# A column roll on one core: the bulk copy's DMA engines take neighbouring rows in place of rows four apart

## The chip, the core and the metric

The kernel runs on one core of one Trainium2 chip. The metric is the device time of one execution in microseconds (us). Lower is better. The core has 16 DMA engines; a DMA that an engine such as SP (SyncE) or ACT (ScalarE) issues goes into that engine's queue, and its packets are worked on by the DMA engines.

## What is computed

The reference rolls every row of an 8192 x 8192 float32 matrix to the right by 100 columns; what leaves a row on the right comes back on its left.

```python
def reference(x: np.ndarray, shift: int) -> np.ndarray:
    return np.roll(x, shift, axis=1)
```

With `shift` 100: out[r, 100:] = x[r, :8092] and out[r, :100] = x[r, 8092:]. Nothing is calculated. The matrix has 268.44 MB, all of which is read from HBM and written to it once. One row has 32,768 bytes, so rows follow each other at 32 KB in both x and out.

## The kernel before

Here s is 100, and a is 256 (line 20 rounds 100 up to 128, line 22 adds 128), so g = a - s is 156. The output's columns are split at a:

- **The bulk**, out[:, 256:8192], is copied straight from x[:, 156:8092], from HBM to HBM (line 43). That is 7936 columns or 31,744 bytes of each row. The rows are taken in 128 blocks of 64 (loop over c, line 39). Inside a block, four DMAs (loop over j, line 41) take 16 rows each: j = 0 and 2 are issued on SP, j = 1 and 3 on ACT (line 43, `engines[j % 2]`). The view of lines 34 and 35 says which 16 rows: its axis e, the outer one of the DMA, has 16 entries, one for each DMA engine. In the last four blocks each DMA is split into two halves of 3968 columns (line 40), so each of the two queues has 248 DMAs of 496 KB and 16 of 248 KB. There is nothing between these DMAs but the wait of a queue for its own earlier DMAs.
- **The heads**, out[:, :256], go through SBUF on the POOL (GpSimd) queue, in 16 groups of 512 rows (loop over k, line 67). A partition holds four rows. Line 72 loads the 256 elements of x that straddle the border between two rows, three times for each partition, into t; lines 73 and 76 load the two pieces that t lacks into h; the DVE (VectorE) copies of lines 74 and 77 bring the rest from t into h in the rolled order. After all loads were issued, line 80 stores the 16 tiles h.

The bulk and the heads write different columns, and no one waits for the other. Both use the same 16 DMA engines.

Rows that DMA j of block c takes, before: c * 64 + 4 * e + j for e = 0 to 15. Entry e's rows over the four DMAs of a block are therefore four in sequence, and neighbouring entries are four rows (128 KB) apart.

Of the kernel before, what the change touches and what calls it, by code (L numbers as in the profile page):

```python
# [1 line left out]

# [4 lines left out]


@with_exitstack
def kernel(  # L10
    ctx: ExitStack,
    tc: tile.TileContext,
    x: bass.AP,
    shift: int,
    out: bass.AP,
):
    nc = tc.nc
    n_rows, n_cols = x.shape
    s = shift % n_cols
    a = -(-s // 128) * 128  # L20
    if 0 < a <= 384 and a + 128 <= n_cols:
        a += 128
    g = a - s
    P = nc.NUM_PARTITIONS
    engines = [nc.sync, nc.scalar]
    n_chunks = 16
    rows = n_rows // n_chunks

    xm = x.rearrange("(c e j) w -> c j e w", e=16, j=4)
    om = out.rearrange("(c e j) w -> c j e w", e=16, j=4)
    if a < n_cols:
        blocks = n_rows // 64
        mid = (a + n_cols) // 256 * 128
        for c in range(blocks):
            parts = ((a, mid), (mid, n_cols)) if c >= blocks - 4 and a < mid else ((a, n_cols),)  # L40
            for j in range(4):
                for lo, hi in parts:
                    engines[j % 2].dma_start(out=om[c, j, :, lo:hi], in_=xm[c, j, :, lo - s:hi - s])
    if a == 0:
        return


    if a > 512:
        for i in range(n_chunks):
            r = slice(i * rows, (i + 1) * rows)  # L50
            nc.gpsimd.dma_start(out=out[r, :s], in_=x[r, n_cols - s:])
            if g > 0:
                nc.gpsimd.dma_start(out=out[r, s:a], in_=x[r, :g])
        return

    Q = 4  # L60
    n_st = n_rows // (P * Q)
    reads = ctx.enter_context(tc.tile_pool(name="reads", bufs=n_st))
    heads = ctx.enter_context(tc.tile_pool(name="heads", bufs=n_st))
    xt = x.rearrange("(k p q) c -> k p q c", q=Q, p=P)
    ot = out.rearrange("(k p q) c -> k p q c", q=Q, p=P)
    tiles = []
    for k in range(n_st):
        t = reads.tile([P, Q - 1, a], x.dtype)
        h = heads.tile([P, Q, a], x.dtype)
        lead = bass.AP(tensor=x.tensor, offset=(k * P * Q + 1) * n_cols - s,  # L70
                       ap=[[Q * n_cols, P], [n_cols, Q - 1], [1, a]])
        nc.gpsimd.dma_start(out=t[:], in_=lead, single_packet=True)  # L72
        nc.gpsimd.dma_start(out=h[:, Q - 1, :s], in_=xt[k, :, Q - 1, n_cols - s:], single_packet=True)  # L73
        nc.vector.tensor_copy(h[:, :Q - 1, :s], t[:, :, :s])  # L74
        if g > 0:
            nc.gpsimd.dma_start(out=h[:, 0, s:], in_=xt[k, :, 0, :g], single_packet=True)  # L76
            nc.vector.tensor_copy(h[:, 1:, s:], t[:, :, s:])  # L77
        tiles.append(h)
    for k, h in enumerate(tiles):
        nc.gpsimd.dma_start(out=ot[k, :, :, :a], in_=h[:], single_packet=True)  # L80


# [1 line left out]
_INS = ['x', 'shift']  # L84
_OUTS = [((8192, 8192), 'float32')]

_NUMBERS = {'shift': 100}


# [26 lines left out]
```

## Time and profile before

| | before |
|---|---|
| median of 3 runs | 817.31 us |
| lowest and highest | 817.02 and 818.74 us |
| profiled execution, its span | 813.9 us |
| instructions in the profile | 689 |
| DMA packets | 22277 |
| bytes moved by the DMA engines | 276.90 MB, mean 340 GB/s |

The profiled execution's own time is its span of 813.9 us, from the first instruction to the last; the runs' times include what lies around the span, 3.4 us between the span and the median. The page counts a byte that goes from HBM to HBM once in "bytes moved", and twice (read and written) in its line on HBM. Whole packets have 31,744 bytes; the many packets under 512 B are 4 bytes long and tell a semaphore that a DMA engine's share of a DMA is done.

The DMA rate over the span, in 40 equal slices of 20.3 us, from the page:

```profile
GB/s 314 346 340 344 353 346 350 344 351 344 346 355 346 345 362 354 353 357 354 355 355 349 342 335 331 335 332 325 335 328 332 334 337 334 332 337 332 334 314 293
```

The first slice holds the start; the last the end, where the queues run empty.

### The profile page before, as it was taken

How to read it: one execution, taken by the hardware profiler on the slowest of the kernel's cores; microseconds unless marked ns; L12 is line 12 of the kernel's file. 1: busy time of each engine (PE TensorE's matmuls, PEld its weight loads, DVE VectorE, ACT ScalarE, POOL GpSimd, SP SyncE). 2: the span in 40 equal slices, each digit the busy share in tenths (PEclk: the TensorE clock that was granted, in tenths of full speed). 3: DMA queues.
4: the chain of work that ended last, by engine and by line, in shares of the span. 5: the costliest groups of instructions: out<-in, count | busy, mean ns of one | idle time of the engine just before them, and what ended most of it. 6: DMA issues, size and time to landing. Idle time of an engine off the chain costs nothing. (4 is left out here: it accounts for less than half of the span.)

```text
span 813.9 us, 689 instructions
## 1 busy us (share of the span) xinstructions
DVE 12.0 (1%) x32; POOL 41.1 (5%) x68
## 2 busy tenths in 40 slices
DVE  0000000000000000000000000000000000000000
POOL 2000011111000100000000000000000000000000
DMA  9999999999999999999999999999999999999998
GB/s 314 346 340 344 353 346 350 344 351 344 346 355 346 345 362 354 353 357 354 355 355 349 342 335 331 335 332 325 335 328 332 334 337 334 332 337 332 334 314 293
DMA packets 22277, 276.90 MB, mean 340 GB/s; under 512 B 9472, under 2 KB 9728, under 8 KB 13824
## 3 DMA queue, kind: packets, MB, share of 16 engines
q1 hardware_dynamic: 8448, 130.04, 45.9%
q10 hardware_dynamic: 8448, 130.04, 44.3%
q0 software_dynamic: 5376, 16.78, 8.9%
q14 instruction: 5, 0.04, 0.0%
HBM read 268.44 MB, written 268.44 MB: 660 GB/s over the span
## 5 line engine op out<-in xcount | busy, mean ns | idle before, releaser
L80 POOL DMA_DIRECT2D out_dram<-h x16 | 11.4, 713 | 139.5 <-DMA out_dram<-h 92.5
L76 POOL DMA_DIRECT2D h<-in_x_dram x16 | 8.6, 540 | 158.4 <-DMA t<-in_x_dram 158.4
L72 POOL DMA_DIRECT2D t<-in_x_dram x16 | 12.2, 760 | 32.1 <-DMA h<-in_x_dram 31.3
L73 POOL DMA_DIRECT2D h<-in_x_dram x16 | 8.9, 558 | 32.7 <-DMA h<-in_x_dram 32.7
L74 DVE COPY h<-t 128x300 f32<-128x300 f32 x16 | 5.9, 367 | 268.4 <-DMA t<-in_x_dram 268.4
L77 DVE COPY h<-t 128x468 f32<-128x468 f32 x16 | 7.5, 468 | 0.0
L97 POOL MEMSET const-float32-0.0<- 128x1 f32 x1 | 0.1, 98 | 0.2 <-issue 0.2
L97 POOL MEMSET const-bfloat16-1.0<- 128x1 bf16 x1 | 0.1, 101 | 0.0
L97 POOL MEMSET const-float32-1.0<- 128x1 f32 x1 | 0.1, 98 | 0.0
L97 POOL MEMSET const-uint8-127<- 128x1 uint8 x1 | 0.1, 98 | 0.0
## 6 DMA issues: line engine op xcount, KB each, us to landing
out_dram<-in_x_dram ACTq DMA_DIRECT2D x248, 496.0 KB, 12.5
out_dram<-in_x_dram SPq DMA_DIRECT2D x248, 496.0 KB, 12.5
out_dram<-h POOLq DMA_DIRECT2D x16, 512.0 KB, 102.9
t<-in_x_dram POOLq DMA_DIRECT2D x16, 384.0 KB, 48.9
out_dram<-in_x_dram SPq DMA_DIRECT2D x16, 248.0 KB, 5.9
out_dram<-in_x_dram ACTq DMA_DIRECT2D x16, 248.0 KB, 5.9
h<-in_x_dram POOLq DMA_DIRECT2D x16, 78.0 KB, 41.9
h<-in_x_dram POOLq DMA_DIRECT2D x16, 50.0 KB, 47.2
```

The source lines that it names most:

```text
L72: nc.gpsimd.dma_start(out=t[:], in_=lead, single_packet=True)
L73: nc.gpsimd.dma_start(out=h[:, Q - 1, :s], in_=xt[k, :, Q - 1, n_cols - s:], single_packet=True)
L74: nc.vector.tensor_copy(h[:, :Q - 1, :s], t[:, :, :s])
L76: nc.gpsimd.dma_start(out=h[:, 0, s:], in_=xt[k, :, 0, :g], single_packet=True)
L77: nc.vector.tensor_copy(h[:, 1:, s:], t[:, :, s:])
L80: nc.gpsimd.dma_start(out=ot[k, :, :, :a], in_=h[:], single_packet=True)
L97: nc = _bacc.Bacc("TRN2", target_bir_lowering=False, num_devices=1)
```

## The change

Two lines are changed, both views of the bulk copy. The order of the axes j and e in the rows of a block is exchanged:

```diff
-    xm = x.rearrange("(c e j) w -> c j e w", e=16, j=4)
-    om = out.rearrange("(c e j) w -> c j e w", e=16, j=4)
+    xm = x.rearrange("(c j e) w -> c j e w", e=16, j=4)
+    om = out.rearrange("(c j e) w -> c j e w", e=16, j=4)
```

DMA j of block c now takes the rows c * 64 + 16 * j + e. Neighbouring entries e take neighbouring rows (32 KB apart), and an entry's next row, in the next DMA, is 16 rows (512 KB) on. Line 43, the number and size of the DMAs, the queues that they are issued on, their order and the heads are as before.

## The prediction

> **What bounds the kernel now.** I read the page's utilisation part first, then its part on DMA queues, then busy time by stretches, then the trace's packet records queue by queue.
>
> The page:
>
> ```profile
> DVE 12.0 (1%) x32; POOL 41.1 (5%) x68
> ...
> DMA  9999999999999999999999999999999999999998
> ...
> q1 hardware_dynamic: 8448, 130.04, 45.9%
> q10 hardware_dynamic: 8448, 130.04, 44.3%
> q0 software_dynamic: 5376, 16.78, 8.9%
> ...
> HBM read 268.44 MB, written 268.44 MB: 660 GB/s over the span
> ...
> out_dram<-in_x_dram ACTq DMA_DIRECT2D x248, 496.0 KB, 12.5
> out_dram<-in_x_dram SPq DMA_DIRECT2D x248, 496.0 KB, 12.5
> ```
>
> No compute engine matters (1% and 5%); the 16 DMA engines are occupied from the first slice to the last. The three queue shares add to 99%. q1 and q10 are the SP and ACT queues with the bulk copy of line 43, q0 is POOL's with the heads. So the kernel is the DMA engines' time, and that is the number of packets times how long one takes.
>
> The stretches (columns: the stretch, its length, DVE busy, POOL busy, tensor clock, DMA share, GB/s):
>
> ```profile
> 100.00:200.00 100.00, 5.26 (x14) 11.57 (x19) 1.00 1.00 349
> 200.00:300.00 100.00, 3.75 (x10) 11.23 (x17) 1.00 1.00 349
> 300.00:400.00 100.00, 0.00 (x0) 4.99 (x7) 1.00 1.01 354
> 400.00:500.00 100.00, 0.00 (x0) 0.71 (x1) 1.00 1.01 346
> 500.00:600.00 100.00, 0.00 (x0) 0.00 (x0) 1.00 1.00 331
> 600.00:700.00 100.00, 0.00 (x0) 0.00 (x0) 1.00 0.99 334
> ```
>
> The DMA share stays at 1.00 while the rate falls from about 349 to 333 GB/s when the heads end near 480 us. The packet records say why. A whole-row packet of 31,744 B takes 1.174 us at the least (27.0 GB/s for an engine), 1.30 us on average from 20 to 250 us and 1.51 us from 500 to 780 us. The engines are occupied, but not at their own speed: something behind them is. A bulk byte is read from HBM and written to HBM; a head's byte touches HBM on one side only, SBUF on the other. Counting bulk bytes twice and head bytes once, 40 us slices carry 651 to 671 GB/s of HBM traffic from 40 us to 800 us. By stage: up to 500 us, (339 + 349 + 349 + 354 + 346) / 5 = 347.4 GB/s in all, 16.78 MB / 500 us = 33.6 of it heads, so 2 x 313.8 + 33.6 = 661; from 500 to 700 us, 2 x 332.5 = 665. Three mixes (bulk with head loads, with head stores, alone) end at one figure within 0.6%. **The bound is HBM traffic at about 663 GB/s**, and 536.9 MB / 813.9 us = 660 is the whole kernel.
>
> The Trainium skill, HBM Reference, Specifications (TRN2), puts one HBM domain at about 716 GB/s; 660 is 92% of that, and the same bytes at 716 would give an estimated 750 us of span, some 753 us in all. The sum below does not use it.
>
> **The change part by part.** Profile to median: the profiled span is 813.9 us, the median of the runs 817.3, so 3.4 us lie around the span; I keep them.
>
> *Removed and added:* nothing. The instruction lists of both kernels are the same on every engine: 264 DMAs on SP, 264 on ACT, 64 on POOL, 32 copies on DVE. Each bulk DMA is still 16 rows, one row for each engine: the queue's 3,968 whole-row packets are 248 DMAs x 16, and each DMA has 16 landings. Sizes, shift and alignment inside a row are unchanged, so the packet count (8448 on a queue) and the 1.174 us floor stay. Issue cost stays: 0.51 us an issue, 264 on a queue, 135 us of 814, and SP waits 667 us in 260 waits for an earlier DMA, so issuing is covered five times over. Cost 0.
>
> *Moved: the rows.* Within each block of 64 rows, DMA j took rows j, j+4, ..., j+60; now it takes 16j to 16j+15. At one moment the two queues touched 32 rows spread over 2 MB of x and of out; now they touch 32 adjacent rows, 1 MB. Neighbouring engines stand 32 KB apart, before 128 KB. An engine that walked four adjacent rows (128 KB nearly in one piece) now steps 512 KB. Three possible costs:
>
> (a) *The loss of the four-row sequence.* If a jump cost something, the packet that begins a group of four would be longer than its followers. I linked packets end to start in the 500 to 780 us stretch (2,843 links of 2,935 packets): the durations four packets apart correlate with 0.004, those two apart with -0.010. A period of four is not there. I take 0 us. If all the scatter above the stretch's median hung on it the mean could move from 1.481 to 1.509, 2%; I keep that in the range.
>
> (b) *Engines meeting on the same part of memory, because rows are a power of two apart.* The start shows the engines in step, one queue after the other, at 128 KB: the first five rounds of 16 packets took 1.62, 1.23, 1.34, 1.52 and 1.37 us on average, the sixth 1.175. Apart from the cold first round and the fourth, this is faster than the free-running 1.51. So standing in step at a power of two is no visible evil at 128 KB; no row has 32 KB in bulk. The heads come nearest: their stores are 1 KB pieces at a 32 KB pitch, and 300 to 480 us, where they run, carries the same 657 to 671 GB/s. I take 0, ends in the rivals.
>
> (c) *Skew among engines.* The 16 landings of one bulk DMA lie some 5 to 7 us apart and four DMAs of a queue are in flight (12.5 us to landing against one every 3.06 us). An engine would have to run 12 us ahead to go idle; the DMA share is 0.99 to 1.00, so this is covered now and stays so unless the skew doubles. Cost 0.
>
> Sum: 813.9 + 0 + 3.4 = 817.3. The ceiling differs by 0.6% between the two stages though the row order in them is the same, so a new order may move it by as much: 0.6% of 814 is 5 us, 812 to 822. Within this band I lean to the slow side, since the ceiling's best slice (671) is 1.2% above its 663 mean and its worst (651) 1.8% below, and say **818**.
>
> **The rivals.**
>
> *B, slower: adjacent rows crowd one part of HBM.* If memory is dealt out by address bits above a row's 32 KB, 32 rows in 1 MB reach fewer parts than 32 rows in 2 MB, and packets that start together wait for one another. For it: packets are 0.34 us over their floor in the pure stage, so waiting is what the time is made of, and the first round, 16 packets within 0.83 us, took 1.62. Against it: (b), and that the engines soon drift out of step. Price: all rounds at 1.62 for 1.51 would be +7.3%, 877 us; the worst warm 40 us slice, 1.533 for 1.509, is +1.6%, 830. I take 830, the row of warm traffic. It decides from about 3% of the rounds meeting like the first (0.2% / 7.3%).
>
> *C, faster: the rows at 32 KB spread better than those at 128 KB.* With all engines on rows of one remainder mod 4, before may have used a quarter of what a low address bit deals out. For it: the same 0.34 us of waiting. Against: engines drift over several j, so all remainders occur already. Price: the best slice kept throughout, 671 GB/s, 536.9 MB / 671 = 800.1, with 3.4 us 803.5; the far end, every whole-row packet at its floor, 7,936 x (1.425 - 1.174) / 16 = 124 us off, 693. I take 803.5, the row that this traffic has reached. The Trainium skill, DMA: Bandwidth & Descriptors, Latency and other measured facts, has copies losing rate as the pitch between streams grows (207 GB/s at 512 KiB, 103 at 4 MiB) and infers that streams in step fall on the same channels; by that rule a smaller pitch can only help. The trace agrees only in that packets wait; its in-step rounds at 128 KB do not show the loss.
>
> *D, the change does not reach the hardware as described.* A packet record carries its queue, not its engine; if the rows were dealt to engines otherwise, nothing would change: 817.3. It ends in the forecast's band and is counted there.
>
> **How the numbers follow.** A measurement of this kernel can tell about 0.2% from no change (its runs span 817.02 to 818.74): 815.7 to 818.9. The forecast (ceiling unmoved, with D) has 0.52, of which 0.20 falls within 0.2%, 0.13 faster, 0.19 slower, by the lean above. B has 0.28: the price of waiting is large and only some collisions are needed. C has 0.20: it needs headroom that only 1.2% of slices' scatter shows. Faster 0.13 + 0.20 = 0.33, same 0.20, slower 0.19 + 0.28 = 0.47. Both signs hold much, so: the forecast's own range is 812 to 822; the whole range goes from just past C's 803.5 to halfway into B's tail, 800 to 845, and leaves out about 0.09 on either side (C towards 693, B towards 877).
>
> **What would show it.** Right: after's pure stage (500 to 700 us) again at 331 to 335 GB/s, q1 and q10 again 45 and 44% in 8448 packets each, DMA digits 9 throughout, the heads ending near 480 us. B: the same DMA share with under 329 GB/s in the pure stage, the mean whole-row packet over 1.53 us. C: over 337 GB/s there, shorter packets. A DMA share well under 1.00 would show (c) wrong; a period of four in packet times, (a). What makes the forecast wrong is above all that HBM's ceiling is not a property of the traffic's volume but of its order, which no stage of before varies in bulk.

## The result, and the profile after

The kernel with the new row order takes **820.99 us** (median of 6 runs, 819.4 to 822.63) against 817.16 us before (6 runs, 816.08 to 818.74): ratio 1.0045, 95% interval 1.003 to 1.0061. It is slower by half a per cent, clear of the 0.2% that can be told. The profiled execution of after has a span of 819.2 us, 5.3 us over before's 813.9. Not all of that is the change. Every run that is recorded with its own span took 1.7 to 1.8 us more than its span, not the 3.4 that lie between before's span and its median. So before's profiled execution took about 815.7 us, 1.5 us under the median of 817.16, while after's, at 821.01 us, was a median one. The difference of the medians, 3.8 us, is the better figure for the change.

The page of after, the lines that answer to those shown of before:

```profile
DVE 12.0 (1%) x32; POOL 41.2 (5%) x68
...
DMA  9999999999999999999999999999999999999988
GB/s 310 344 346 346 352 348 345 341 352 348 349 329 353 346 356 353 354 350 356 348 351 354 355 342 330 332 328 335 319 324 324 324 321 324 332 329 333 343 293 299
...
q1 hardware_dynamic: 8448, 130.04, 46.2%
q10 hardware_dynamic: 8448, 130.04, 44.1%
q0 software_dynamic: 5376, 16.78, 8.9%
...
HBM read 268.44 MB, written 268.44 MB: 655 GB/s over the span
...
out_dram<-in_x_dram ACTq DMA_DIRECT2D x248, 496.0 KB, 12.6
out_dram<-in_x_dram SPq DMA_DIRECT2D x248, 496.0 KB, 12.6
```

Packets, bytes, issues and the engines' occupation are what they were: the same packets in the same queues, 99% of 16 engines' time. Only the rate has changed, 655 for 660 GB/s of HBM traffic. The row of GB/s says where: its first 23 values look like before's, and from the middle of the span on, after the heads, most lie at 319 to 335 where before had 325 to 337. The stretches of after at the same places (columns as before: length, DVE, POOL, tensor clock, DMA share, GB/s):

```profile
100.00:200.00 100.00, 3.76 (x10) 9.94 (x16) 1.00 1.00 347
200.00:300.00 100.00, 3.76 (x10) 10.19 (x16) 1.00 1.00 346
300.00:400.00 100.00, 0.75 (x2) 5.70 (x8) 1.00 1.01 353
400.00:500.00 100.00, 0.00 (x0) 2.14 (x3) 1.00 1.00 349
500.00:600.00 100.00, 0.00 (x0) 0.00 (x0) 1.00 1.00 329
600.00:700.00 100.00, 0.00 (x0) 0.00 (x0) 1.00 1.00 324
```

While heads and bulk run together, after moves 346 to 353 GB/s, as before did. From 500 us, where the bulk is all but alone (after has 0.13 MB of heads left), it moves 329 and 324 where before moved 331 and 334, at the same DMA share of 1.00. The packet records give the account in bytes: at 480 us after has copied 150.02 MB of the bulk and before 149.92, so the bulk has lost nothing yet (the heads are 0.3 MB behind, 16.37 against 16.68, and their last packet ends at 543 us, before at 504); at 780 us it is 248.01 against 249.72 MB. The missing 1.71 MB are 5.1 us at 332.5 GB/s, practically the whole 5.3 between these two executions. A whole-row packet took 1.54 us on average from 500 to 700 us, 1.51 before; the shortest take 1.173 us in both.

So between these two executions the change costs some 1.6% of the stage in which the bulk is alone (110 MB in 339.2 us, before 333.9), by the medians 1.1% (3.8 of 333.9 us). In the stage with heads it costs the bulk nothing that shows.

### The profile page after: what moved, and what is told of

Same layout as the page of the kernel before. It is cut to its first block, busy times and chain, and to the rows that moved or that the text cites. A ratio compares the mean times of both kernels' runs of the same rounds, so it can differ in the third digit from the quotient of the medians.

```text
span 819.2 us, 689 instructions
## 1 busy us (share of the span) xinstructions
DVE 12.0 (1%) x32; POOL 41.2 (5%) x68
## 4 chain that ended last, share of the span: by engine, by line
DMA 31%; another core or an unknown queue 19%; POOL 1%; issue 1%; POOLq 0%; PEldq 0%
DMA h<-in_x_dram 27%; DMA t<-in_x_dram 4%; POOL out_dram L80 1%; POOL h L73 0%; POOL t L72 0%; POOLq L111 0%; POOL h L76 0%; POOLq L80 0%; PEldq L111 0%
## 6 DMA issues: line engine op xcount, KB each, us to landing
out_dram<-in_x_dram ACTq DMA_DIRECT2D x248, 496.0 KB, 12.6
out_dram<-in_x_dram SPq DMA_DIRECT2D x248, 496.0 KB, 12.6
```

## The experiments

Two theories at the start. *Theory 1:* an engine loses by stepping 16 rows, in place of four adjacent rows in sequence. *Theory 2:* rows that are copied at the same time crowd HBM when they are only 32 KB apart. To see an effect of 1.6% of one stage well, the heads are left out in most kernels: the bulk then runs alone throughout. All diffs are against the kernel before. Each ratio is to the kernel before (with heads) on the same chip.

### The two orders alone

Both leave out the heads:

```diff
-    if a == 0:
-        return
...
+    return
```

> The kernel before with the heads left out (columns 0 to 255 of the output are not written), so that the bulk copy runs alone throughout, in the old row order. 260.05 MB at the 332.5 GB/s of the stage in which before's bulk ran alone is 782 us, and some 7 us for start and end: 789 us by every theory. It is the base for the other three.

> The same without heads, in the new row order. If the loss of 2% in the stage where the bulk runs alone (326 for 332 GB/s) is the order's own, it now acts on the whole span: 260.05 MB / 326 = 798, with start and end 805 us, 2% over the kernel in the old order. If it needs the heads (their packets leave the engines in a worse step), both are equal within 0.3%.

bulk_adj has the two changed lines as well. Measured: old order 790.03 us (ratio 0.9673, 95% interval 0.966 to 0.9687), new order 803.61 (0.9838, 0.9811 to 0.9866), 1.7% slower. The new order's runs also scatter more: 798.2 to 807.7 us, the old order's 789.24 to 791.85. The loss is the order's own and needs no heads. It is there early, too: at 480 us the new order has copied 155.7 MB, the old one 158.3, where the whole kernels were level. So the loss does not show while the heads' traffic runs beside the bulk. The stretch 40 to 700 us, old order, then new (columns here: length, POOL, tensor clock, DMA share, GB/s):

```profile
40.00:700.00 660.00, 0.00 (x0) 1.00 1.00 331
```

```profile
40.00:700.00 660.00, 0.00 (x0) 1.00 1.00 327
```

The engines are equally occupied, at 331 against 327 GB/s.

### The sequence taken away, the spacing kept

```diff
-        for c in range(blocks):
...
-            for j in range(4):
...
+        for n in range(4 * blocks):
+            c, j = n % blocks, n // blocks
...
+                engines[n % 2].dma_start(out=om[c, j, :, lo:hi], in_=xm[c, j, :, lo - s:hi - s])
```

> Without heads. Neighbouring engines four rows apart as before, but the four rows of an engine come in four passes over the matrix (loop over j outside of the loop over blocks), so that no engine copies two adjacent rows one after the other. Theory 1, the four-row sequence is what was lost: as slow as the new order, about 805 us. Theory 2, rows 32 KB apart at the same time crowd HBM: as fast as the old order, about 789 us, or faster.

Measured: 786.2 us (785.97 to 786.34), ratio 0.9629 (0.9616 to 0.9641): faster than the old order, not slower. **Theory 1 falls.** From one DMA to the next an engine steps 64 rows here, and the kernel is the fastest of the set. Its rate from 40 to 700 us is 334 GB/s:

```profile
40.00:700.00 660.00, 0.00 (x0) 1.00 0.99 334
```

Why it beats the old order by 0.45% stays open: two things differ, the sequence, and that SP's and ACT's rows no longer adjoin on one engine.

### Read side and write side apart

```diff
-    om = out.rearrange("(c e j) w -> c j e w", e=16, j=4)
+    om = out.rearrange("(c j e) w -> c j e w", e=16, j=4)
```

and its counterpart, with xm changed and om kept.

> Without heads. x is read in the old order, out is written in the new one (so rows are exchanged within each block of 64 in the output). If the read side alone makes the loss, 789 us; if the write side alone does, 805 us; if each has half, about 797 us; if the loss comes from reads and writes that follow one another on the same row of both tensors, something else, since that relation is broken here.

> Without heads, the counterpart of the kernel that read in the old order and wrote in the new (802.4 us, as slow as the new order on both sides): x is read in the new order, out is written in the old one, rows again exchanged within a block of 64. Theory W, the spacing of the rows being written makes the loss: about 790 us, like the old order. Theory R, any mismatch or any 32 KB spacing, on the read side too, makes it: about 802 us.

Measured: reads old, writes new 802.37 us (0.9825, 0.9807 to 0.9843), like the new order on both sides (0.9838). Reads new, writes old 789.22 us (0.9656, 0.9639 to 0.9673), like the old order on both (0.9673). **The loss is made on the write side alone**; the source rows may be adjacent at no cost. The same stretch, first writes new, then writes old:

```profile
40.00:700.00 660.00, 0.00 (x0) 1.00 1.00 328
```

```profile
40.00:700.00 660.00, 0.00 (x0) 1.00 0.99 333
```

The loss is not the same all the time. In the one profile of the kernel that writes in the new order and reads in the old, it lies early: 327 GB/s from 40 to 300 us against 333 in the old order (bulk_seq4), but 331 against 331 from 500 to 700 us. Why it fades there is not shown.

### The two queues apart

```diff
-    om = out.rearrange("(c e j) w -> c j e w", e=16, j=4)
+    om = out.rearrange("(c e j) w -> c j e w", e=16, j=1)
...
+            c, j = n % 2 * (blocks // 2) + n // 2, 0
```

(xm likewise, blocks of 16 rows, and the single loop over n of above.)

> Without heads, neighbouring engines on neighbouring rows as in the new order, but SP copies the upper half of the matrix and ACT the lower half, so that the two queues' rows stand 4096 rows apart and not 16. If it is the spacing among the 16 rows of one DMA that costs, about 803 us, like the new order. If it is that all rows in flight lie in one stretch (32 to 128 adjacent rows), two stretches should bring back part of it, under 797 us.

Measured: 801.6 us (0.981, 0.9788 to 0.9831), not to be told from the new order's 0.9838. Putting half of the active rows 4096 rows away brings back nothing that shows. The close rows of one DMA are enough:

```profile
40.00:700.00 660.00, 0.00 (x0) 1.00 1.00 327
```

### Other spacings

xm and om with j = 2, 8 or 16 rows between neighbouring engines, as many passes over the matrix, and blocks of 16 j rows (shown for 16; the single loop over n as above):

```diff
-    om = out.rearrange("(c e j) w -> c j e w", e=16, j=4)
+    om = out.rearrange("(c e j) w -> c j e w", e=16, j=16)
...
-        blocks = n_rows // 64
+        blocks = n_rows // 256
```

> Without heads, neighbouring engines 16 rows (512 KB) apart, the 16 rows of an engine in 16 passes. Theory 2 (rows close together crowd HBM) by spacing alone: no slower than 786 us at 4 rows. The Trainium skill's rule on row pitch at large powers of two would have it slower than at 128 KB, if streams at 512 KB already meet: over 790 us.

> Without heads, neighbouring engines 2 rows (64 KB) apart, two passes. With 803.6 us at 1 row, 786.2 at 4 and 827.6 at 16, a curve with one lowest point between would put this at 786 to 803 us, about 795. If the loss at 1 row is special to adjacent rows, it is as fast as 4 rows, about 786.

> Without heads, neighbouring engines 8 rows (256 KB) apart, eight passes. A curve with one lowest point puts this between 786 and 828 us, about 805; if the loss at 16 rows is special to 512 KB, it is at 786 or below, and the whole kernel should take it.

| rows between neighbouring engines | KB | us | ratio to before, 95% interval |
|---|---|---|---|
| 1 (the new order) | 32 | 803.61 | 0.9838 (0.9811 to 0.9866) |
| 2 | 64 | 787.63 | 0.9642 (0.9627 to 0.9657) |
| 4 | 128 | 786.2 | 0.9629 (0.9616 to 0.9641) |
| 8 | 256 | 791.29 | 0.9681 (0.9667 to 0.9695) |
| 16 | 512 | 827.55 | 1.0124 (1.0106 to 1.0142) |

The guesses of a smooth curve (about 795 us at 2 rows, 805 at 8) missed. From 64 to 256 KB the times lie within 0.7%, though 8 rows are slower than 4 by 0.5%, clear of the intervals, and so miss the other guess of 786 us or below too. Outside there is a step at either end: of the spacings tried, the loss at 1 row is special to adjacent rows, and the larger loss at 16 rows is another. The stretch at 2, 8 and 16 rows:

```profile
40.00:700.00 660.00, 0.00 (x0) 1.00 1.00 333
```

```profile
40.00:700.00 660.00, 0.00 (x0) 1.00 1.00 331
```

```profile
40.00:700.00 660.00, 0.00 (x0) 1.00 1.00 317
```

The next kernel reads x at 512 KB and writes out at 128 KB:

```diff
+    xm = x.rearrange("(c e j) w -> c j e w", e=16, j=16)
+    om = out.rearrange("(c i e j) w -> c i j e w", e=16, i=4, j=4)
...
+                engines[n % 2].dma_start(out=om[c, j // 4, j % 4, :, lo:hi], in_=xm[c, j, :, lo - s:hi - s])
```

> Without heads, x is read with 16 rows between engines, out is written with 4 (rows exchanged within blocks of 256), in 16 passes. If the written rows' spacing alone sets the rate, as between 1 and 4 rows: 786 to 790 us. If at 512 KB the reads suffer too: over 800, up to 828 us.

Measured: 825.12 us (1.0104, 1.0087 to 1.012). With writes at 128 KB it is still slow, so at 512 KB the reads bring the loss, where at 32 KB the writes did. (Writes at 512 KB beside reads at 128 KB were not tried.) These are two costs on two sides:

```profile
40.00:700.00 660.00, 0.00 (x0) 1.00 0.99 318
```

One thing goes along with the spacing in the table: the step from a DMA's rows to those of the next one, 512 KB at 1 row and 8 MB at 16. At 32 KB, bulk_adj_far speaks against the step as the cause: its consecutive DMAs lie in different halves of the matrix, and it is as slow. For the reads at 512 KB, spacing and step were not parted.

### Adjacent rows, or always the same remainder

With adjacent rows an engine also stays on rows of one remainder mod 16 for good. Groups of 17 rows, of which 16 are copied, were to part the two:

```diff
+    xm = x[:8177].rearrange("(c e) w -> c e w", e=17)
+    om = out[:8177].rearrange("(c e) w -> c e w", e=17)
...
+                engines[n % 2].dma_start(out=om[c, :16, lo:hi], in_=xm[c, :16, lo - s:hi - s])
```

> Without heads, and with every 17th row left out (481 groups of 17 rows, 16 of them copied by neighbouring engines): 7,696 rows, 244.3 MB. Neighbouring engines still write adjacent rows at the same time, but an engine no longer stays on rows of one remainder mod 16; each group turns it on by one. If adjacent rows in flight are the loss: the rate of the new order, (803.6 - 9) x 7696 / 8192 + 9 = 755 us. If the loss is that an engine stays on the same remainder: the rate of 2 to 4 rows' spacing, (786.2 - 9) x 0.9395 + 9 = 739 us, up to 743 (from 790.0).

Measured: 749.83 us (748.29 to 752.75; ratio 0.9168, 0.9142 to 0.9195), between the two expectations (755; 739 to 743). This is **inconclusive**: scaled to all rows it is (749.83 - 9) / 0.9395 + 9 = 797.5 us, so turning brings back some 6 (by the intervals 3 to 9) of the 14 to 17 us of loss, and the engine's step of 17 rows is a further difference.

```profile
40.00:700.00 660.00, 0.00 (x0) 1.00 1.00 329
```

The runs of the table say more about the remainder. In the passes at 2, 4 and 8 rows an engine also stays on rows of one remainder mod 16, for a whole pass (at 4 rows it takes the rows c * 64 + 4 * e + j with j fixed), and these are the fast kernels. So staying on one remainder is not by itself the loss. What the memory does with adjacent rows is not settled.

### A version with heads

The whole kernel with the bulk in four passes at 4 rows, the diff of bulk_pitch4_noseq, heads kept:

> The whole kernel with heads, the bulk in the order that was the fastest alone (engines four rows apart, four passes over the matrix: 786.2 us against 790.0 for the old order without heads). In before and after the order told only in the stage where the bulk runs alone, some 330 of 814 us. So 3.8 us x 330 / 785 = 1.6 us gained of it: about 815 us against 816 to 817. If the order tells in the mixed stage too, 812 to 813.

Measured: 815.21 us (812.82 to 816.48, 10 runs) against 817.26 before: 0.9971 (0.9958 to 0.9984). It beats both kernels, before by 2 us (interval 1.3 to 3.4) where 1.6 were worked out from the kernels without heads. Where it gains them is not shown: its profiled execution has 333 GB/s from 500 to 700 us, as before's has.

## Why the prediction was right, and where it was off

- **By its own signs it was rival B that came, not the forecast.** The forecast wanted 331 to 335 GB/s from 500 to 700 us; rival B under 329, and whole-row packets over 1.53 us on average. After has 329 and 324 in the two halves of that stretch and packets of 1.54 us. The total fell into the forecast's band; the mechanism behind the sum, an unmoved ceiling, did not hold.
- **The bound.** Right in kind: the engines are occupied, but their packets take longer than the 1.173 us that the shortest take, so something behind the engines sets the time. All runs kept the DMA share near 1.00 and differed in packet length (on average from 40 to 700 us: 1.51 us with four rows between engines in passes, 1.54 with one, 1.59 with 16). Wrong was that the traffic's volume alone fixes it, at about 663 GB/s.
- **Nothing added or removed.** Right: same packets, same issues, same queue shares within 0.3 points.
- **(a) the four-row sequence, 0 us.** Right, and shown: without it the bulk alone was faster (786.2 against 790.0 us). That packet durations four apart correlated with 0.004 agrees with it.
- **(b) engines meeting on a part of memory, 0 us.** This is the term that was mis-sized. It is 3.8 us in the medians and 5.3 us in the profiled spans, of which 1.5 are due to a fast profiled execution of before; the 1.7% of the kernels without heads would be 5.7 us of the 333.9 us in which the bulk runs alone. Its reasoning failed in two places. The rounds in step at 128 KB said nothing of 32 KB, and the heads' stores at a 32 KB pitch, which "come nearest", ran in the stage where the order of the bulk does not tell either (after kept before's rate there). What the prediction named last as its weak point is so: the ceiling depends on the order, and by order alone the rate of the bulk without heads went from 317 to 334 GB/s.
- **The 3.4 us around the span.** The time around the span is 1.8 us; the other 1.6 is how far before's profiled execution lay under the median of then, 817.31 us. The sum comes out at the median either way.
- **(c) skew among engines, 0 us.** Right: the DMA share of the alone stage stayed at 0.99 to 1.00, and a queue's DMA lands in 12.6 us for 12.5.
- **Rival B** named the mechanism that came (rows close together crowd HBM) and priced it at 830 us. Its place was too wide: in the kernels without heads the loss is on the writes only, beside the heads it does not show, which leaves 334 us in place of 814, and 16 adjacent rows of one DMA do it without the other queue's 16. 1.6% over the whole span would have been its 13 us; over 334 us it is 5.3. Its premise that engines which start together wait for one another was not tested.
- **Rival C** failed: a smaller spacing than 128 KB brings no gain, neither at 64 KB (787.6 against 786.2 us, intervals overlapping) nor at 32. The Trainium skill, DMA: Bandwidth & Descriptors, Latency and other measured facts, gives rates that fall as the pitch grows from 512 KiB to 4 MiB, and no figure below that. Here a growing spacing costs time from 128 to 512 KB as well (786.2 to 827.6 us; at 512 KB it is the reads that bring the loss). That "a smaller pitch can only help" was the prediction's extension of it, and the runs contradict it from 64 to 32 KB (787.6 to 803.6 us), where the writes lose; the measurement decides.
- **Rival D** (the order does not reach the hardware) failed as far as this shows: the order alone moves the bulk's time. Which engine took which row is not in the records, so "neighbouring engines" is by the program throughout.
- **The lean to the slow side** was right in sign by luck: its reason, that the worst slice lay farther from the mean than the best, had nothing to do with the cause. That the time fell into the forecast's band of 812 to 822 was luck too, since it came through a cost that the sum had at 0 and that the heads kept small.

## What to carry to other kernels

When DMA engines are occupied all the time but their packets take longer than the shortest ones do, as here (1.51 against 1.173 us), look for the limit behind the engines, and test on its own which rows are in flight together, reads and writes apart: here 64 to 256 KB between engines was good, 32 KB bad for writes, 512 KB bad for reads. Measure such an effect with the other traffic left out: beside heads with 8.9% of the engines' time over the whole span, the bulk's loss did not show. A row of the profile taken under other traffic is not the nearest row for a cost in the stage without it.

## What the runs showed of the hardware that was not expected

- The cost of an order is not the same for reads and writes: writes at 32 KB between engines cost 1.6% with reads at 128 KB (0.9825 / 0.9673) and 1.9% with reads at 32 KB (0.9838 / 0.9656), reads at 32 KB nothing that shows; reads at 512 KB, with a step of 8 MB to the next DMA's rows, cost 4.9% (1.0104 / 0.9629).
- A bulk copy's loss, 1.7% without heads, did not show while 16.8 MB of other packets ran beside it (150.02 against 149.92 MB at 480 us, one execution each). Why is open; that the heads' packets keep the engines from standing side by side was not tried.
